# All projection weights of the last mixer as one sequence of tiles prepared two ahead, in four pairs of buffers

## The chip, the cores and the metric

The kernel runs on one core of a Trainium2 chip. The metric is the device time of one execution in microseconds (us); several runs give a median. Besides the times there is one profiled execution of the kernel before, with the start, the length and the releaser of the instructions of every engine: TensorE (PE in the profile; its weight loads are PEld), VectorE (DVE), ScalarE (ACT), GpSimd (POOL) and SyncE (SP), whose queue issues the DMAs.

## The reference, cut to what matters

The program computes two blocks on one sequence of 256 positions of width 1024, in fp32. The first block is a mixer and an MLP; the second has two layers, each a mixer and an MLP. The change touches the mixer of the very last layer, an RWKV-7 mixer:

```python
def _rwkv7_mixer(h, mu, w_rkv, w0, w_la, w_lb, a0, a_la, a_lb, g_la, g_lb,
                 k_k, k_a, r_k, ln_g, ln_b, w_o, v_first, v_mix):
    ...
    xx = jnp.pad(h, ((0, 0), (1, 0), (0, 0)))[:, :-1] - h
    xs = h[None] + xx[None] * mu[:, None, None, :]
    rkv = jnp.einsum('pbtd,pde->pbte', xs[:3], w_rkv)
    r, k, v = rkv[0], rkv[1], rkv[2]
    ...
    decay = jnp.exp(-jnp.exp(log_w.astype(f32)))
    ...
    a = jax.nn.sigmoid(a0 + (xa @ a_la) @ a_lb)
    g = jax.nn.sigmoid(xg @ g_la) @ g_lb
    kk = heads(k * k_k).astype(f32)
    kk = kk / jnp.maximum(jnp.sqrt(jnp.sum(kk * kk, axis=-1, keepdims=True)), 1e-12)
    k = k * (1.0 + (a - 1.0) * k_a)
    ...
    y = _wkv7_scan(r_h, heads(decay), k_h, v_h, kk, kk * heads(a).astype(f32))
    ...  # normalised per head, bonus added, times g
    return y.astype(h.dtype) @ w_o, v_first
```

The weights `w_rkv` are three 1024 x 1024 matrices, for r, k and v. The recurrence is computed in four windows of 64 positions, in two halves d = 0 and 1; inside a window a triangular system is solved by an elimination.

## The kernel before, in words

**Split arithmetic.** Every fp32 product is made of three matmuls on halves: a high half, which is the value rounded to the type fp32r, and a low half, which is the rest. `mm3` issues high x high, high x low and low x high (L227 to L229). A weight tile of 128 x 1024 goes through `split`: ACT writes the high half with a cast (L222), then DVE or POOL writes the low half with a subtraction (L223). In the names of the profile wk is the raw tile of a k weight, wkh and wkl its halves, and wr, wrh, wrl and wv, wvh, wvl the same for r and v; m1u, m2u and m3u are weights of the three MLPs. The pair of halves lies in one of two buffers of the pool `wp`; the raw 1 MB tile, which holds two split tiles, in one of two buffers of `wr`. A split can start when its raw tile has landed and the pair that it takes is no longer read by TensorE; a load can start when the raw buffer that it takes is no longer read by a split. Outside this mixer, `more_weights` lends two further pools, and then splits and loads alternate between the pools (the list `extra`).

**The last mixer** is the function `rwkv`. In its order of code: the input is normalised to hT by TensorE and ACT (rn, L1231 and L1235); xx is the difference to the position before (L1325); mixes of hT and xx are the inputs of the projections; `k_proj(0)` to `k_proj(3)` each load 256 columns of the k weights in one DMA, split them in two tiles and make two 128-column products, whose squares sq and their sums kk give the norms nk. `lora_b` loads the small matrix lwab into a raw buffer between `k_proj(0)` and `k_proj(1)`. After `k_proj(3)` an inverse square root over 128 x 32 values (`rsqrt`, L275 to L284, tiles nr and nt) gives the factors that ACT widens to ly (L1390) and TensorE turns into tile nk of PSUM (L1394); with them DVE and POOL make tA, tB and tK (tAR and tBK hold them). `r_proj(0)` and `r_proj(1)` stand between these steps; each `r_proj` ends in lx<-r and tAR<-r on DVE (L1414, L1415), the first two also in operations on tK.

**The elimination and its fill.** `blocks` makes the small blocks (AB), DVE solves them in 16 steps per half: in a step for half 0 DVE does the work, for half 1 POOL makes the product elp (`elp` = "dp", L921) and DVE adds it to hT (L924). Then come the pieces Pc, Zc, Rc and Uc on TensorE. While DVE eliminates, TensorE has its fill: the generator `dense` gives `r_proj(2)`, `r_proj(3)`, the bonus sums (bon, from pr, which is lx), and the eight tiles' v matmuls of the first half, `v_proj(0)`, with A (gram, L1469) between; `late` gives `v_proj(1)` and the gate (G). `v_out` writes V (L1529). At the end `fin` normalises the output per head (gv, gr, gt, tBK, L1699 to L1710), adds the bonus and multiplies by the gate; yt is its transpose for the product with `w_o`, yh and yl the halves of that, ra and res the residual sum, and then the last MLP starts with its weights m3u.

**Which engine splits.** The table `KP` names the engine of each low half: k "dd,dd,dd,dd" (all DVE), r "dp,pd,dd,pd" (POOL has r1, r2 and r6, counted from 0) and v "d,d,d,p,d,d,p,p" (POOL has v3, v6 and v7). The change leaves it as it is.

**What sets the order.** Each engine runs its instructions in the order that a scheduler has laid down when the program is built. It orders by priority and by when operands and buffers come free, so the place of a split in an engine's queue follows from the number of buffers too, and it is not the order of the code. An instruction that waits holds up all behind it on its engine.

## Time and profile before

| what | us |
|---|---|
| median of three runs | 1083.26 (1081.01, 1083.26, 1083.73) |
| the profiled execution | 1082.76 |
| its span in the trace | 1081.0 |
| PE busy in the span | 1044.6 (97%) |
| DVE busy | 734.9 (68%) |
| ACT busy | 553.0 (51%) |
| POOL busy | 71.2 (7%) |

The profiled execution took 1.8 us more than the span of its trace. The stage of the last mixer lies from about 620 to 880 us of the span. [...] A wait is put down to the releaser that came last; what that releaser was itself held up by has to be read from its engine.

### The profile page before, as it was taken

The numbers are of one execution on the slowest core, as the hardware profiler recorded it, in microseconds if no ns is written. First come the engines' busy times: TensorE is split into PE (matmuls) and PEld (weight loads), VectorE is DVE, ScalarE is ACT, GpSimd is POOL, SyncE is SP. The second block draws the span as 40 slices with busy tenths as digits, with TensorE's granted clock in tenths as the row PEclk, the third lists the DMA queues.
The fourth block names the chain that finished last, engine by engine and source line by source line (L and its number), as shares of the span: only waits on it lengthen the run. The fifth ranks groups of instructions, "written<-read, shape, count | busy, mean of one in ns | idle before, by whom it ended". The sixth has DMA issues, their size and how long they took to land.

```text
span 1081.0 us, 19651 instructions
## 1 busy us (share of the span) xinstructions
PE 1044.6 (97%) x8138; PEld 936.9 (87%) x8138; DVE 734.9 (68%) x1269; ACT 553.0 (51%) x826; POOL 71.2 (7%) x100
## 2 busy tenths in 40 slices
...
GB/s 245 122 157 118 45 343 196 195 162 189 160 211 139 215 157 194 160 172 185 156 273 194 179 154 47 98 105 92 60 99 112 86 156 158 193 195 187 187 133 40
DMA packets 113910, 169.44 MB, mean 157 GB/s; under 512 B 6446, under 2 KB 92443, under 8 KB 113564
## 3 DMA queue, kind: packets, MB, share of 16 engines
...
q8 instruction: 64, 1.05, 0.4%
...
q10 hardware_dynamic: 146, 0.07, 0.0%
HBM read 167.12 MB, written 1.05 MB: 156 GB/s over the span
## 4 chain that ended last, share of the span: by engine, by line
PE 82%; DVE 12%; ACT 3%; issue 2%; DMA 1%; POOL 1%; ACTq 0%; POOLq 0%; DVEq 0%
PE m1a L227 3%; PE m3h L228 3%; PE m3h L229 3%; PE m1a L229 3%; PE m1a L228 3%; PE m3h L227 3%; PE m1h L228 3%; PE m2h L228 3%; PE m2h L229 3%; PE m1h L229 3%; PE m1h L227 3%; PE m2h L227 3%; PE m2a L227 3%; PE m2a L228 3%; PE m2a L229 3%; PE m3a L227 3%
## 5 line engine op out<-in xcount | busy, mean ns | idle before, releaser
L227 PE MATMUL m1h<-m1xh,m1uh 128*128 128x256 f32 x256 | 73.4, 287 | 0.0
L229 PE MATMUL m3h<-m3xh,m3ul 128*128 128x256 f32 x256 | 72.3, 283 | 0.5 <-DVE m3ul L223 0.5
L228 PE MATMUL m3h<-m3xl,m3uh 128*128 128x256 f32 x256 | 72.2, 282 | 0.3 <-DVE m3xl L387 0.3
L227 PE MATMUL m3h<-m3xh,m3uh 128*128 128x256 f32 x256 | 72.1, 282 | 0.0
L228 PE MATMUL m1h<-m1xl,m1uh 128*128 128x256 f32 x256 | 71.9, 281 | 0.2 <-DVE m1xl L387 0.2
L229 PE MATMUL m2h<-m2xh,m2ul 128*128 128x256 f32 x256 | 71.7, 280 | 0.0
L229 PE MATMUL m1h<-m1xh,m1ul 128*128 128x256 f32 x256 | 71.7, 280 | 0.0
L228 PE MATMUL m2h<-m2xl,m2uh 128*128 128x256 f32 x256 | 71.7, 280 | 0.0
L223 DVE TENSOR_TENSOR m3ul<-m3u,m3uh 128x1024 fp32r<-128x1024 f32 x32 | 39.2, 1226 | 47.6 <-ACT m3uh L222 47.6
L227 PE MATMUL m2h<-m2xh,m2uh 128*128 128x256 f32 x256 | 71.6, 280 | 0.0
L223 DVE TENSOR_TENSOR m1ul<-m1u,m1uh 128x1024 fp32r<-128x1024 f32 x32 | 39.2, 1225 | 44.8 <-ACT m1uh L222 44.8
L223 DVE TENSOR_TENSOR m2ul<-m2u,m2uh 128x1024 fp32r<-128x1024 f32 x32 | 39.1, 1225 | 35.9 <-ACT m2uh L222 35.9
L222 ACT CAST m3uh<-m3u 128x1024 fp32r<-128x1024 f32 x32 | 33.5, 1047 | 53.9 <-PE m3h L228 50.0
L222 ACT CAST m1uh<-m1u 128x1024 fp32r<-128x1024 f32 x32 | 33.7, 1053 | 52.1 <-PE m1h L228 50.4
L222 ACT CAST m2uh<-m2u 128x1024 fp32r<-128x1024 f32 x32 | 33.5, 1050 | 47.9 <-PE m2h L228 45.4
L223 DVE TENSOR_TENSOR m2dl<-m2d,m2dh 128x1024 fp32r<-128x1024 f32 x32 | 39.2, 1224 | 26.1 <-ACT m2dh L222 26.1
L223 DVE TENSOR_TENSOR m3dl<-m3d,m3dh 128x1024 fp32r<-128x1024 f32 x31 | 38.0, 1225 | 24.9 <-ACT m3dh L222 24.9
L223 DVE TENSOR_TENSOR m1dl<-m1d,m1dh 128x1024 fp32r<-128x1024 f32 x31 | 37.9, 1224 | 22.0 <-ACT m1dh L222 22.0
L222 ACT CAST m2dh<-m2d 128x1024 fp32r<-128x1024 f32 x32 | 33.6, 1050 | 33.4 <-PE m2a L229 29.9
L222 ACT CAST m1dh<-m1d 128x1024 fp32r<-128x1024 f32 x31 | 32.5, 1047 | 35.3 <-PE m1a L229 24.4
L227 PE MATMUL m2a<-m2dh,m2fh 128*128 128x512 f32 x128 | 50.1, 391 | 0.0
L228 PE MATMUL m2a<-m2dl,m2fh 128*128 128x512 f32 x128 | 49.9, 390 | 0.0
...
## 6 DMA issues: line engine op xcount, KB each, us to landing
m1u<-in_w_up_dram SPq DMA_DIRECT2D x16, 1024.0 KB
m1d<-in_w_down_dram SPq DMA_DIRECT2D x16, 1024.0 KB, 4.9
m2u<-in_ffn_w_dram SPq DMA_DIRECT2D x16, 1024.0 KB, 6.6
m2d<-in_ffn_w_dram SPq DMA_DIRECT2D x16, 1024.0 KB, 5.6
m3u<-in_ffn_w_dram SPq DMA_DIRECT2D x16, 1024.0 KB, 5.6
m3d<-in_ffn_w_dram SPq DMA_DIRECT2D x16, 1024.0 KB, 4.8
win<-in_w_in_dram SPq DMA_DIRECT2D x10, 1024.0 KB
sv<-in_sgu_w_in_dram SPq DMA_DIRECT2D x8, 1024.0 KB, 6.9
```

Source lines behind the costliest of these rows:

```text
L222: act.copy(hv, src)
L223: lo.tensor_tensor(out=lv, in0=src, in1=hv.bitcast(F32), op=ALU.subtract)
L227: pe.matmul(out, lhsT=lh, rhs=rh, start=first, stop=False)
L228: pe.matmul(out, lhsT=lh, rhs=rl, start=False, stop=False)
L229: pe.matmul(out, lhsT=ll, rhs=rh, start=False, stop=last)
```

## The change

In `rwkv` a pool `wz` of two further pairs is opened and put on `extra` (with no raw pool beside it), so splits alternate between `wp` and `wz`, four pairs in all, until the end of `rwkv`, where it is popped. The SBUF for it is what `dynamic_dma_scratch_size=1024` gives up. The weights of k, r and v become one sequence of 24 tiles, k0 to k7, r0 to r7, v0 to v7. `prep(i)` loads and splits tile i (a raw tile for every second one); `tile_of(m, u, ahead)` prepares all tiles up to two beyond the one that is asked for (`k_proj(0)` asks with ahead=1) and returns it. Two further differences lie in the loads. A raw tile of k or r weights comes as two DMAs of 128 columns each in place of one of 256 columns; v weights come as four DMAs of 1 MB in place of eight of 512 KB. The branch for `lo == "x"` and the engine "x" are not reached, since `KP` names no "x".

```diff
--- before.py
+++ after.py
@@ -136,7 +136,7 @@
     act, dve, pool, pe, sync = nc.scalar, nc.vector, nc.gpsimd, nc.tensor, nc.sync
 
     cp = ctx.enter_context(tc.tile_pool(name="const", bufs=1))
-    EN = {"d": dve, "p": pool, "a": act}
+    EN = {"d": dve, "p": pool, "a": act, "x": "x"}
 
     def scale_by(e, out, in_, cols):
         if e is act:
@@ -178,7 +178,7 @@
 
     def raw(name):
         wpick[1] += 1
-        w_ = extra[-1][1] if extra and wpick[1] % 2 and not wpick[2] else wr
+        w_ = extra[-1][1] if extra and extra[-1][1] and wpick[1] % 2 and not wpick[2] else wr
         return w_.tile([P, 2048], F32, tag="raw", name=name)
 
     def load_ws(w, c0, name, n=256):
@@ -220,7 +220,11 @@
             hv = hv.rearrange("p (a b) -> p a b", a=shape[1])
             lv = lv.rearrange("p (a b) -> p a b", a=shape[1])
         act.copy(hv, src)
-        lo.tensor_tensor(out=lv, in0=src, in1=hv.bitcast(F32), op=ALU.subtract)
+        if lo == "x":
+            act.activation(out=lv, in_=hv.bitcast(F32), func=AF.Copy, scale=-1.0)
+            pool.dma_start(out=lv.bitcast(F32), in_=src, accum_op=ALU.add)
+        else:
+            lo.tensor_tensor(out=lv, in0=src, in1=hv.bitcast(F32), op=ALU.subtract)
         return hv, lv
 
     def mm3(out, lh, ll, rh, rl, first, last):
@@ -1143,7 +1147,38 @@
     def rwkv(fed, early, cols, mu, hcol, hka, laf):
         NP, CH = 8, 64
         half = 0.5 * DECAY
-        with tc.tile_pool(name="rw", bufs=1) as bp:
+        with tc.tile_pool(name="wz", bufs=2) as wz, tc.tile_pool(name="rw", bufs=1) as bp:
+            extra.append((wz, None))
+            w3 = a["rwkv_w_rkv_2"][0]
+            made, src = {}, {}
+            how = [KP[x].replace(",", "") for x in ("rk", "rr", "rv")]
+
+            def prep(i):
+                if i > 23 or i in made:
+                    return
+                m, u = divmod(i, 8)
+                if u % 2 == 0:
+                    t = raw(f"w{'krv'[m]}{u}")
+                    if m < 2:
+                        v = t.rearrange("p (j k c) -> p j k c", j=2, k=NK)
+                        for j in range(2):
+                            sync.dma_start(out=v[:, j], in_=w3[1 - m][:, (u + j) * P:(u + j + 1) * P]
+                                           .rearrange("(k p) c -> p k c", p=P))
+                        src[i], src[i + 1] = v[:, 0], v[:, 1]
+                    else:
+                        v = t.rearrange("p (j k c) -> p j k c", j=2, k=2)
+                        n, c = divmod(u, 4)
+                        sync.dma_start(out=t.rearrange("p (k c) -> p k c", k=4),
+                                       in_=w3[2][c * 256:c * 256 + 512, n * 512:n * 512 + 512]
+                                       .rearrange("(k p) c -> p k c", p=P))
+                        src[i], src[i + 1] = v[:, 0], v[:, 1]
+                made[i] = split(src.pop(i), "w" + "krv"[m], EN[how[m][u]])
+
+            def tile_of(m, u, ahead=2):
+                for i in range(8 * m + u + ahead + 1):
+                    prep(i)
+                return made[8 * m + u]
+
             nkeep = _O2["reset2"][0]
             cc = bp.tile([P, nkeep], F32, tag="cc2", name="cc2")
             sync.dma_start(out=cc, in_=a["c2"][:, :nkeep])
@@ -1201,7 +1236,6 @@
                 xx = xxf.rearrange("p (k t) -> p k t", k=NK)
                 mixf = m2.tile([P, 2, 1024], F32, tag="mix", name="mix", bufs=1)
                 sqf = m2.tile([P, 2, 512], F32, tag="sq", name="sq", bufs=1)
-                w3 = a["rwkv_w_rkv_2"][0]
 
                 xh, xl, _, part = fed
                 pool.memset(hT[:, :, 0:1], 0.0)
@@ -1286,8 +1320,7 @@
                 nk = mp.tile([P, 2, 2 * NP], F32, tag="nk", name="nk")
 
                 def k_proj(c, kh, kl):
-                    w = load_ws(w3[1], c * 256, f"wk{c}")
-                    hl = [split(w[:, :, j * P:(j + 1) * P], "wk", EN[KP["rk"].split(",")[c][j]]) for j in range(2)]
+                    hl = [tile_of(0, 2 * c + j, 2 if c else 1) for j in range(2)]
                     q = lin("k")
                     qv = q.rearrange("p (j t) -> p j t", j=2)
                     if c == 0:
@@ -1401,11 +1434,10 @@
                     EN[KP["tk"][1]].tensor_tensor(out=tK[:, s], in0=tK[:, s], in1=as4(tt[:, s]), op=ALU.mult)
 
                 def r_proj(c):
-                    w = load_ws(w3[0], c * 256, f"wr{c}")
                     q = lin("r")
                     qv = q.rearrange("p (j t) -> p j t", j=2)
                     for j in range(2):
-                        wh, wl = split(w[:, :, j * P:(j + 1) * P], "wr", EN[KP["rr"].split(",")[c][j]])
+                        wh, wl = tile_of(1, 2 * c + j)
                         for k in range(NK):
                             mm3(qv[:, j], wh[:, k], wl[:, k], rh[:, k], rl[:, k], k == 0, k == NK - 1)
                             if k % 2:
@@ -1510,9 +1542,7 @@
                     ac = gv[2]
                     m = slice(n * 512, n * 512 + 512)
                     for c in range(4):
-                        w = raw(f"wv{n}{c}")[:, :1024].rearrange("p (k c) -> p k c", k=2)
-                        sync.dma_start(out=w, in_=w3[2][c * 256:c * 256 + 256, m].rearrange("(k p) c -> p k c", p=P))
-                        wh, wl = split(w, "wv", EN[KP["rv"].split(",")[4 * n + c]])
+                        wh, wl = tile_of(2, 4 * n + c)
                         for j in range(2):
                             k = 2 * c + j
                             for t in range(2):
@@ -1798,6 +1828,7 @@
                     add_res(ac[1], 1, n, None)
                 for n in range(2):
                     fed[2](1, n)
+            extra.pop()
             return fed
 
     with more_weights(1, 1):
@@ -1876,7 +1907,7 @@
     import concourse.bacc as bacc
     from concourse.bass_utils import run_bass_kernel_spmd
 
-    nc = bacc.Bacc("TRN2", target_bir_lowering=False, num_devices=1)
+    nc = bacc.Bacc("TRN2", target_bir_lowering=False, num_devices=1, dynamic_dma_scratch_size=1024)
     arrays = {n: np.ascontiguousarray(inputs[n]) for n in _INS}
     arrays["c1"], arrays["c2"] = _C1, _C2
     arrays = {f"in_{n}_dram": v for n, v in arrays.items()}
```

What the diff alone does not show is how the queues stand afterwards. The lines of the kernel after are by 4 higher up to the head of `rwkv` and by 30 to 34 further down.

The first place is DVE's queue at the inverse square root nr, behind the last k projection. Before, from the first operation of the chain on:

```order
L284 TENSOR_SCALAR nr_7429<-nk_6995 128x32
L275 TENSOR_TENSOR nt_7430<-nr_7429 128x32
L276 TENSOR_TENSOR nt_7430<-nt_7430,nk_6995 128x32
L282 SCALAR_TENSOR_TENSOR nt_7430<-nt_7430 128x32
L282 SCALAR_TENSOR_TENSOR nr_7429<-nt_7430,nr_7429 128x32
L275 TENSOR_TENSOR nt_7430<-nr_7429 128x32
L1270 TENSOR_TENSOR mvl_7605<-mix_6824,mvh_7604 128x4x256
L276 TENSOR_TENSOR nt_7430<-nt_7430,nk_6995 128x32
L1414 TENSOR_TENSOR lx_6997<-r_7452,tBK_6809 128x512
L282 SCALAR_TENSOR_TENSOR nr_7429<-nt_7430,nr_7429 128x32
L1415 TENSOR_TENSOR tAR_6808<-r_7452,EL_6820 128x4x2x64
L223 TENSOR_TENSOR wrl_7554<-wr1_7522,wrh_7553 128x1024
```

After, at the same place; here the chain begins in the sixth row, and the splits are r3, r4 and r5 (the row tAR<-k and the mvl rows stood ahead of the rows shown before):

```order
L227 TENSOR_TENSOR wrl_7501<-wr2_7469,wrh_7500 128x1024
L1340 TENSOR_TENSOR tAR_6811<-k_7382,rwcols_5575 128x4x128
L1304 TENSOR_TENSOR mvl_7625<-mix_6827,mvh_7624 128x4x256 x2
L1349 TENSOR_SCALAR nk_6998<-kk_7434 128x2x4
L227 TENSOR_TENSOR wrl_7546<-wr4_7542,wrh_7545 128x1024
L288 TENSOR_SCALAR nr_7447<-nk_6998 128x32
L1446 TENSOR_TENSOR lx_7000<-r_7468,tBK_6812 128x512
L279 TENSOR_TENSOR nt_7448<-nr_7447 128x32
L1447 TENSOR_TENSOR tAR_6811<-r_7468,EL_6823 128x4x2x64
L280 TENSOR_TENSOR nt_7448<-nt_7448,nk_6998 128x32
L227 TENSOR_TENSOR wrl_7574<-wr4_7542,wrh_7573 128x1024
L286 SCALAR_TENSOR_TENSOR nt_7448<-nt_7448 128x32
```

Before, r3's split is the last row, behind the two operations that end r(0), and the chain has no split in it. Now r3, r4 and r5 stand in front of the chain and within it. TensorE's queue moves with it: ahead of its first nk it had, between the sums kk, 25 and 23 and 16 matmuls of r, and has now 33 and 15 and 41; the 48 matmuls of r(3) (24 a tile) now all stand before bon. Further up on DVE, k1's split, the product sel and k3's split stand ahead of xx, where k1 and sel stood, and k2 takes the place of k1; on ACT the casts of k1 and k3 stand before the first hT.

The second place is POOL's queue in the elimination; wvl are the splits of v tiles, elp the products of the steps 10 to 15 of half 1. Before:

```order
L921 TENSOR_TENSOR elp_8092<-elb_8073,hT_6822 128x16x10
L921 TENSOR_TENSOR elp_8131<-elb_8127,hT_6822 128x16x11
L223 TENSOR_TENSOR wvl_8227<-wv03_8224,wvh_8226 128x1024
L921 TENSOR_TENSOR elp_8176<-elb_8157,hT_6822 128x16x12
L921 TENSOR_TENSOR elp_8235<-elb_8211,hT_6822 128x16x13
L921 TENSOR_TENSOR elp_8260<-elb_8256,hT_6822 128x16x14
L921 TENSOR_TENSOR elp_8294<-elb_8284,hT_6822 128x16x15
L223 TENSOR_TENSOR wvl_8474<-wv12_8471,wvh_8473 128x1024
```

After:

```order
L925 TENSOR_TENSOR elp_8150<-elb_8146,hT_6825 128x16x11
L925 TENSOR_TENSOR elp_8195<-elb_8176,hT_6825 128x16x12
L227 TENSOR_TENSOR wvl_8321<-wv6_8318,wvh_8320 128x1024
L925 TENSOR_TENSOR elp_8252<-elb_8230,hT_6825 128x16x13
L925 TENSOR_TENSOR elp_8277<-elb_8273,hT_6825 128x16x14
L925 TENSOR_TENSOR elp_8311<-elb_8301,hT_6825 128x16x15
L227 TENSOR_TENSOR wvl_8405<-wv6_8318,wvh_8404 128x1024
```

Before, v3's split stands between the products 11 and 12, and v6's behind the last; now v3 stands behind the product 2 (further up than the rows shown), v6 between 12 and 13 and v7 behind the last. Also on POOL, r1 and r2 are now neighbours, and r6 stands ahead of the operations on tBK and xx that precede the elimination. On DVE the splits among the steps of the elimination were r7, v0, v1, v2 and v4 and are v0, v1, v2, v4 and v5, and the operations lx and tAR that end r(3) stand behind step 2, where they stood behind step 5. On TensorE 22 matmuls of v stand before the first piece of Pc, where 13 stood.

The third place is the end of `fin` on DVE, from the last product with V of one half to the last yl. Before:

```order
L1710 TENSOR_TENSOR tBK_6809<-tBK_6809,V1_7975 128x512
L275 TENSOR_TENSOR gt_9279<-gr_9278 128x8
L345 TENSOR_TENSOR res_79<-ra0_9266,res_79 128x512
L276 TENSOR_TENSOR gt_9279<-gt_9279,gv_9277 128x8
L345 TENSOR_TENSOR res_79<-ra0_9266,res_79 128x512
L282 SCALAR_TENSOR_TENSOR gr_9278<-gt_9279,gr_9278 128x8
L252 TENSOR_TENSOR yl_8842<-yt_9340,yh_8841 128x4x128
L1708 TENSOR_TENSOR tBK_6809<-tBK_6809,gr_9278 128x512
L1709 TENSOR_TENSOR tBK_6809<-tBK_6809,G1_7974 128x512
L1710 TENSOR_TENSOR tBK_6809<-tBK_6809,V1_7975 128x512
L223 TENSOR_TENSOR m3ul_9497<-m3u0_9494,m3uh_9496 128x1024
L252 TENSOR_TENSOR yl_8842<-yt_9359,yh_8841 128x4x128
```

After:

```order
L1739 TENSOR_TENSOR tBK_6812<-tBK_6812,G1_7995 128x512
L286 SCALAR_TENSOR_TENSOR gr_9281<-gt_9282,gr_9281 128x8
L349 TENSOR_TENSOR res_79<-ra0_9269,res_79 128x512
L1740 TENSOR_TENSOR tBK_6812<-tBK_6812,V1_7996 128x512
L1738 TENSOR_TENSOR tBK_6812<-tBK_6812,gr_9281 128x512
L349 TENSOR_TENSOR res_79<-ra0_9269,res_79 128x512
L1739 TENSOR_TENSOR tBK_6812<-tBK_6812,G1_7995 128x512
L256 TENSOR_TENSOR yl_8845<-yt_9343,yh_8844 128x4x128
L1740 TENSOR_TENSOR tBK_6812<-tBK_6812,V1_7996 128x512
L256 TENSOR_TENSOR yl_8845<-yt_9362,yh_8844 128x4x128
L227 TENSOR_TENSOR m3ul_9505<-m3u0_9498,m3uh_9504 128x1024
```

The split of m3u0's first tile, which stood between the two yl, is no longer in the rows: it stands further up, between gv and gr of the last normalisation. The row below the second yl is the split of m3u0's second tile. A res row now stands before V.

## Rows read from the trace of the kernel before

**Rows 1.** The chain that ended last, share of the span by engine.

```profile
PE 82%; DVE 12%; ACT 3%; issue 2%; DMA 1%; POOL 1%; ACTq 0%; POOLq 0%; DVEq 0%
```

**Rows 2.** TensorE's waits, 620 to 900: engine, line, releaser: us, times, longest.

```profile
PE A L1469 <- DVE lx L1473: 2.4, 1, 2.4
PE nk L1394 <- ACT ly L1390: 1.6, 1, 1.6
...
PE v L227 <- DVE V L1529: 1.3, 2, 0.7
PE kk L1314 <- ACT sq L1310: 1.1, 1, 1.1
PE r L229 <- POOL wrl L223: 0.9, 1, 0.9
PE k L229 <- DVE wkl L223: 0.8, 1, 0.8
...
PE yt L248 <- DVE gt L275: 0.4, 1, 0.4
```

**Rows 3.** Windows: length; busy PE, PEld, DVE, ACT, POOL; clock, DMA, GB/s.

```profile
720.00:740.00 20.00, 17.36 (x366) 16.15 (x367) 19.73 (x32) 7.66 (x12) 5.14 (x5) 1.00 0.31 98
728.00:732.00 4.00, 4.00 (x36) 4.00 (x36) 3.97 (x7) 1.88 (x4) 0.00 (x0) 1.00 0.76 251
752.00:756.00 4.00, 4.00 (x22) 3.94 (x21) 1.89 (x15) 0.00 (x0) 0.86 (x3) 0.57 0.70 228
760.00:780.00 20.00, 17.65 (x132) 14.01 (x131) 19.41 (x59) 10.69 (x27) 5.83 (x8) 0.99 0.25 80
```

**Rows 4.** Tile wk: its splits, shortest/mean/longest in ns, from and to.

```profile
L222 ACT CAST wkh<-wk x8: 1039/1052/1056, 651.8 to 707.2; 128x1024 fp32r<-128x1024 f32 x8
L223 DVE TENSOR_TENSOR wkl<-wk,wkh x8: 1202/1220/1254, 652.9 to 709.9; 128x1024 fp32r<-128x1024 f32 x8
```

**Rows 5.** Timeline of DVE: start, length, line, operation, idle time before.

```profile
720.08 2.31 DVE L275 TENSOR_TENSOR nt<-nr 128x32 f32<-128x32 f32 x1
722.42 0.19 DVE L276 TENSOR_TENSOR nt<-nt,nk 128x32 f32<-128x32 f32 x1
...
739.81 2.85 DVE L1574 TENSOR_TENSOR hT<-xx,cc 128x512 f32<-128x512 f32 x1
...
756.50 0.69 DVE L1414 TENSOR_TENSOR lx<-r,tBK 128x512 f32<-128x512 f32 x1 [2.57 <-PE r L229]
...
772.21 3.05 DVE L924 TENSOR_TENSOR hT<-hT,elp 128x176 f32<-128x176 f32 x2
```

**Rows 6.** Timeline of POOL: two weight splits.

```profile
719.97 2.38 POOL L223 TENSOR_TENSOR wrl<-wr,wrh 128x1024 fp32r<-128x1024 f32 x1
...
794.77 2.37 POOL L223 TENSOR_TENSOR wvl<-wv,wvh 128x1024 fp32r<-128x1024 f32 x1 [7.79 <-ACT wvh L222]
```

**Rows 7.** Timeline of TensorE: first and last of 20 matmuls of k.

```profile
704.43 0.28 PE L227 MATMUL k<-mkh,wkh 128*128 128x256 f32 x1
...
706.66 0.28 PE L228 MATMUL k<-mkl,wkh 128*128 128x256 f32 x1
```

**Rows 8.** Timeline of TensorE: first and last of 15 matmuls of 512 columns.

```profile
639.80 0.39 PE L227 MATMUL m2a<-m2dh,m2fh 128*128 128x512 f32 x1
...
642.97 0.39 PE L229 MATMUL m2a<-m2dh,m2fl 128*128 128x512 f32 x1
```

**Rows 9.** Timeline of DVE at xx, ahead of the k projections.

```profile
669.87 1.23 DVE L1325 TENSOR_TENSOR xx<-hT 128x1024 f32<-128x1024 f32 x1 [2.40 <-ACT hT L1235]
```

**Rows 10.** Timeline of ACT at its first hT.

```profile
666.00 2.17 ACT L1235 ACTIVATE hT<-rn,gcols 128x128 f32<-128x128 f32 x8 [2.80 <-PE rn L1231]
```

**Rows 11.** Timeline of DVE in fin.

```profile
869.81 0.17 DVE L284 TENSOR_SCALAR gr<-gv 128x8 int32<-128x8 int32 x1
...
873.37 0.69 DVE L1710 TENSOR_TENSOR tBK<-tBK,V 128x512 f32<-128x512 f32 x1
```

**Rows 12.** DMA from 518 to 523.6, and issues from 620 to 830: KB, us.

```profile
DMA packets 3120, 1.05 MB, mean 187 GB/s; under 512 B 2096, under 2 KB 3120, under 8 KB 3120
...
wk<-in_rwkv_w_rkv_dram SPq DMA_DIRECT2D x4, 1024.0 KB, 5.1
```

## Prediction

> **What bounds the kernel now.** The chain of work that ended last comes first: TensorE holds 82% of it, DVE 12% [rows 1], so only time in which TensorE stands still, or runs slower, can be won. All edits lie in the last mixer, so I read TensorE's waits from 620 to 900 us [rows 2]. Two name a weight split: k<-DVE wkl (0.8 us) and r<-POOL wrl (0.9). Four more up to the end of v_out(0) name neighbours: nk<-ACT ly 1.6, kk<-ACT sq 1.1, A<-DVE lx 2.4, v<-DVE V 1.3. The stretches say why: DVE is busy 19.73 of 20 us from 720 to 740 and 19.41 from 760 to 780 [rows 3]; there TensorE waits for DVE's queue, whatever name the last releaser has. So the second question is what lengthens that queue. First, splits of 1.22 us [rows 4]. Second, instructions held up beside POOL: nt<-nr, a 128x32 operation, takes 2.31 us against 0.19 for its successor, hT<-xx 2.85 against 0.69 for an lx<-r of the same size, hT<-hT 3.05 for two [rows 5]; a POOL split of about 2.4 us runs beside the first, and its like beside the others [rows 6]. Third, a stop of 2.57 us before lx<-r [rows 5], where DVE's head waits for the r projection.
>
> A matmul of a k or r projection starts every 0.117 us (20 of them, 704.43 to 706.66) [rows 7], one of 512 columns every 0.226 (15, 639.80 to 642.97) [rows 8].
>
> **The change, part by part.** I write k0 to v7 for the 24 split tiles. Engines, sizes and numbers of splits and matmuls stay the same; no engine is spared work, it only moves.
>
> *Splits ahead of the stage.* k1 and k3 now stand on DVE around sel, before xx. DVE was idle for 2.40 us there [rows 9], and two splits are 2 x 1.22 = 2.44; ACT, which casts them before its first hT, was idle 2.80 us [rows 10]. So k3 costs nothing, nor does k1, which stood a little earlier, and k2 takes k1's old place. If that cover is short, xx and all behind it are late by some tenths. From there each split position of the k projections holds the tile two further on, so DVE's packed part begins with two splits fewer: -2.4 us. k6's split is done long before its matmuls, so the 0.8 of [rows 2] goes: -0.8. The load of lwab, in k1's raw buffer, now waits for k1's split, and its cast stands behind the hT and mix casts on ACT: 0.
>
> *The nr chain* (first order fence). r3, r4 and r5 stand in or before it, where r3 followed it. Ahead of the first nk TensorE now has 33+15+41 = 89 matmuls of r instead of 25+23+16 = 64: 25 x 0.117 = 2.9 us of work in place of the waits of 0.9 and 1.6. That counts only if the nr chain comes no later. For it: r2's POOL split, beside which nt<-nr lost 2.31 - 0.19 = 2.1 [rows 5], is ready earlier. Against it: r1 and r2 then run beside the two lv instructions and r3. I take half, -1.0; bounds 0 and -2.1. ACT's casts of r4 to r6 stand before the ly copies and wait for buffers: r6's for r2's, free after 24 of the 41 matmuls, so it ends before ly is due.
>
> *The elimination.* From the first AB evacuation to the last transposes DVE does v0, v1, v2, v4, v5 where it did r7, v0, v1, v2, v4; against the two splits taken off at the start, the packed part holds one more at its end (v5): +1.2. POOL's r6 now runs before the AB evacuation, so the 2.85 - 0.69 = 2.2 that hT<-xx lost [rows 5] goes, unless r6 hits the tA and tB work instead; half, -1.1 (0 to -2.2). The 2.57 stop goes if r(3) is done when lx comes: TensorE has the 0.8 + 0.9 + 1.6 = 3.3 us from above in hand and does all of r(3) before bon, but lx also stands three steps earlier; -2.0 (0 to -2.6). POOL's v6, which ran at 794.77 with DVE out of its way [rows 6], now stands between elp 12 and elp 13 (second fence). Its nearest row is v3, in the same kind of place: hT<-hT took 3.05 for two [rows 5]. So at most it costs the length of a POOL split, 2.4 [rows 6], in which POOL's next elp waits too; at least 0.3, a little overlap. I take 2.3, nearest to v3. v3 itself moves from step 11 to step 2, at its old price.
>
> Sum on DVE at the end of the elimination: -2.4 - 0.8 + 1.2 - 1.0 - 1.1 - 2.0 + 2.3 = -3.8. The best bounds give -8.6, but TensorE can't win more than its waits there, 0.8 + 0.9 + 1.6 + 2.4 + 1.3 = 7.0; the worst give +0.4.
>
> *Before Pc.* Nine v matmuls that stood between the Pc and Zc pieces come ahead of the first Pc, so TensorE fills with them what it would wait for X: 9 x 0.226 = 2.0, -2.0. It is 0 if the pieces behind then lack cover; eight or more v matmuls still stand before Zc, so I take -2.0. Together -5.8 of the 7.0.
>
> *fin and m3u0.* w_out's splits 2 and 3 now take one pair from either pool, so m3u0's first split finds a buffer early, and DVE's queue gets it, 1.22 as in [rows 4], between gv and gr of the last normalisation. DVE has no gap there from gr at 869.81 to V at 873.37 [rows 11], and TensorE already waits 0.4 for yt [rows 2]: yt comes 1.2 later, later again by the res operation that now stands before V (0.69, as V's last [rows 11]) (third fence), and yl behind further operations. Against that, m3ul is there later on. I take +1.8, bounds 0 and +2.4.
>
> *DMA.* k and r weights come as two loads of 128-column pieces, in rows of 512 bytes where one load had 1024. Landing took 5.1 us for 1 MB [rows 12]; at twice the packets the bound is 10.2. The nearest row is the load of la: 1.05 MB in 3120 packets, 2096 of them under 512 bytes, all between 518 and 523.6 us [rows 12]; so 5.1 to 6. The tightest is r6: its load can start once r3 is split, 1.05 + 1.22 = 2.3 us [rows 4] after the last k matmul; its cast is due 72 r matmuls after that, 72 x 0.117 = 8.4; 6.1 us of room, so nothing waits. The scratch given up holds nothing of this kernel, which starts no DMA on POOL's queue: 0.
>
> [...]
>
> **Sum.** 1082.76 (the profiled execution; the median is 0.5 above it) - 3.8 - 2.0 + 1.8 = 1078.8.
>
> **Rivals.**
> *Given back on DVE:* the waits named by weights go, but the packed queue, with v6 inside and r1, r2 beside lv, ends where it ended, and the waits come back as A<-DVE and Pc<-DVE: 0 - 2.0 + 1.8: 1082.6. For it: no DVE work is saved, 19.73 of 20 [rows 3]. Against: two splits and the 2.57 stop do leave it.
> *No weight is late:* TensorE's two weight waits are 1.7 us in all [rows 2]; if only they go and fin costs 1.8, 1082.9. I count it with the last.
> *Late landing, slower:* if 1 MB in 512-byte rows takes over 6.1 us, r6's cast heads ACT's queue ahead of ly, and nk waits. At 10.2 it is 4.1 late, about 7 with r4's load on the same queue still running when r6's starts; that is some 4 beyond TensorE's extra 2.9 of work. DVE's -3.8 turns to about +2.9; then -2.0 + 1.8; and the clock, at 0.57, mostly its lower level, from 752 to 756, lets through 22 matmuls where 728 to 732 has 36 [rows 3], (36 - 22) x 0.117 = 1.6 more after such a stop: 1087. Against it stands the load of la.
> *More:* if that stretch at 0.57 goes as well, all 7.0 are won and fin is free: -7.0 - 1.6: 1074.2.
>
> **How the numbers follow.** Forecast 0.60 (1075.5 to 1081.5), given back and no weight late 0.24, slower 0.09, more 0.07. A measurement of this kernel tells about 0.3% from no change, 3.25 us: faster ends at 1080.0, slower begins at 1086.5. Some four fifths of the forecast lie below 1080.0: 0.49 + 0.07 = 0.56 faster; 0.09 slower; 0.35 within. The range leaves out the slower rival and most of the last one: 1074.8 to 1084.4.
>
> **What would show it.** Right: no wait on wkl or wrl; first nk with no wait; DVE's last transposes of the elimination 3 to 5 us earlier; a POOL wvl between two elp with DVE held up beside it; yt<-DVE at 1.5 to 2 us near the end. Wrong: casts waiting for a DMA, an nr chain as late as before, lx<-r still stopping DVE, or Pc waiting over 3 us for DVE.

## The result, and the profile after

The changed kernel is slower. Its median is 1093.24 us (four runs, 1091.22 to 1094.80) against 1082.76 for the kernel before (1081.01 to 1083.73); the ratio is 1.0095, with a 95% interval of 1.0079 to 1.0112. The forecast was 1078.8, with a range of 1074.8 to 1084.4 and a chance of 0.09 for slower; the median lies 8.8 us above that range. The profiled execution of the changed kernel took 1091.22 us (span 1089.4), that of before 1082.76 (span 1081.0). Four single runs of the experiments below were disturbed and took 2584 to 3851 us (one each of before, e7, e9 and e15); they stand in no ratio, and in a median they count for less than 0.1 us.

The medians differ by 10.5 us, the two profiled executions by 8.5. Nothing happens outside the last mixer. I cut both traces at the same instructions of TensorE: the last m2a, the first AB (the elimination begins), the first Pc, the last Zc, the first Rc, the first yt of `fin` and the first m3h of the MLP. Between the cuts, in us:

| part | before | after | difference |
|---|---|---|---|
| last m2a to first AB (projections, nr chain) | 73.83 | 77.10 | +3.27 |
| first AB to first Pc (elimination) | 57.42 | 56.20 | -1.22 |
| first Pc to last Zc | 17.73 | 19.14 | +1.41 |
| last Zc to first Rc | 8.50 | 8.37 | -0.13 |
| first Rc to first yt | 42.14 | 43.57 | +1.43 |
| first yt to first m3h (`fin`) | 30.74 | 34.81 | +4.07 |
| sum | 230.36 | 239.19 | +8.83 |

The parts do not hold the same work. Of the 192 matmuls of r, 101 stand ahead of the first AB before and 117 after, and of the 96 of v, 58 and 67 stand ahead of the first Pc. At 0.117 us for one of r and 0.226 for one of v [rows 7, 8], 1.9 us of work moved from the second part to the first, and 2.0 from the third to the second. For the same work, then, the differences of the first three parts are about +1.4, -1.4 and +3.4. And one execution is a coarse measure: e1_fin, e3_v7_dve and e4_v_between_pc (below) have the changed kernel's order on every engine up to the first AB, and their first parts took 75.7, 75.5 and 78.1.

TensorE's waits of the changed kernel from 620 to 910, releaser, us, times and longest, answer to [rows 2]:

```profile
PE kk L1347 <- ACT sq L1343: 3.6, 2, 2.4
PE Pc L1621 <- issue: 2.5, 1, 2.5
PE Pc L1621 <- DVE xx L1614: 2.2, 1, 2.2
PE yt L252 <- DVE tBK L1740: 1.9, 1, 1.9
PE v L231 <- DVE V L1559: 1.8, 1, 1.8
...
PE A L1501 <- DVE lx L1505: 0.2, 1, 0.2
```

What the change was made for did happen. The waits on wkl (0.8) and wrl (0.9) and nk<-ACT ly (1.6) are gone, and A<-DVE lx fell from 2.4 to 0.2: 5.5 us of waiting won. But kk<-ACT sq grew from 1.1 to 3.6, v<-DVE V from 1.3 to 1.8, yt's from 0.4 to 1.9, and two stops before and in Pc are new, 2.2 and 2.5: 9.2 lost.

In the part from the first Rc to the first yt, which grew by 1.4, a stop before Uc without a releaser lasted 1.4 in place of 0.7, and Uc waited 0.6 for sq.

The second loss is not in a list of waits. These are stretches of the changed kernel (length; busy PE, PEld, DVE, ACT, POOL; granted clock of TensorE as a share of full speed, DMA share, GB/s), to be read beside [rows 3]:

```profile
716.00:720.00 4.00, 1.55 (x14) 1.35 (x13) 4.00 (x10) 1.67 (x3) 0.40 (x1) 1.00 0.30 73
720.00:724.00 4.00, 4.00 (x20) 4.00 (x20) 2.30 (x4) 0.33 (x1) 0.00 (x0) 0.50 0.88 238
724.00:728.00 4.00, 4.00 (x25) 4.00 (x24) 3.61 (x8) 1.05 (x1) 1.27 (x1) 0.64 0.00 2
796.00:800.00 4.00, 2.33 (x41) 1.55 (x41) 0.20 (x1) 0.00 (x0) 0.00 (x0) 0.50 0.01 4
880.00:884.00 4.00, 3.20 (x10) 2.10 (x11) 2.98 (x5) 0.59 (x1) 0.00 (x0) 0.56 0.00 0
884.00:888.00 4.00, 4.00 (x14) 3.29 (x13) 1.92 (x2) 1.53 (x2) 0.00 (x0) 0.59 0.37 90
```

From 716 to 720 TensorE works 1.55 of 4 us, and in the 8 us behind that the granted clock is 0.50 and 0.64: it is never idle there, but 20 and 25 matmuls pass where the kernel before passes 36 at 1.00 [rows 3]. The same follows the stop in Pc and the one before yt. Summed as (1 - clock) x 4 us over the stretches of 4 us from 660 to 904, before lacks 12.0 us of full clock and after 20.5. I take that as an upper bound on what the clock cost, since it counts waits within such stretches as well. Weighted with the time that TensorE was busy it is 11.1 and 18.4, 7.3 more; but that too may be more than it cost: in `fin` below, 3.4 us of lacking clock cost about 2.2. So waits and clock make up the 8.8 together: all idle time of TensorE between the cuts, named here or not, grew from 15.6 to 20.2 us, 4.6, and its matmuls were busy for 219.0 us in place of 214.8, 4.2 more for the same work.

### The profile page after: what moved, and what is told of

Same layout as the page of the kernel before. It is cut to its first block, busy times and chain, and to the rows that moved or that the text cites. A ratio compares the mean times of both kernels' runs of the same rounds, so it can differ in the third digit from the quotient of the medians.

```text
span 1089.4 us, 19653 instructions
## 1 busy us (share of the span) xinstructions
PE 1049.8 (96%) x8138; PEld 940.9 (86%) x8138; DVE 736.5 (68%) x1269; ACT 552.7 (51%) x826; POOL 72.2 (7%) x100
## 4 chain that ended last, share of the span: by engine, by line
PE 82%; DVE 11%; ACT 2%; issue 2%; DMA 1%; POOL 1%; SPq 0%; ACTq 0%; POOLq 0%; DVEq 0%
PE m1a L231 3%; PE m3h L232 3%; PE m3h L233 3%; PE m1a L233 3%; PE m1a L232 3%; PE m3h L231 3%; PE m1h L232 3%; PE m2h L232 3%; PE m2h L233 3%; PE m1h L233 3%; PE m2h L231 3%; PE m1h L231 3%; PE m2a L231 3%; PE m2a L232 3%; PE m2a L233 3%; PE m3a L231 3%
## 5 line engine op out<-in xcount | busy, mean ns | idle before, releaser
L232 PE MATMUL m3h<-m3xl,m3uh 128*128 128x256 f32 x256 | 72.1, 282 | 0.3 <-DVE m3xl L391 0.3
L231 PE MATMUL m3h<-m3xh,m3uh 128*128 128x256 f32 x256 | 72.1, 282 | 0.0
L222 ACT CAST m3uh<-m3u 128x1024 fp32r<-128x1024 f32 x32 | 33.6, 1049 | 51.7 <-PE m3h L232 51.7
L222 ACT CAST m2dh<-m2d 128x1024 fp32r<-128x1024 f32 x32 | 33.6, 1050 | 33.4 <-PE m2a L233 28.1
```

What stands on the lines that cost most here:

```text
L222: act.copy(hv, src)
L231: pe.matmul(out, lhsT=lh, rhs=rh, start=first, stop=False)
L232: pe.matmul(out, lhsT=lh, rhs=rl, start=False, stop=False)
```

## The experiments

From this trace I named four causes: **POOL's hold-up** (r1 and r2 run back to back beside small DVE operations, so kk is late and the clock falls), **v7** (POOL's last v split beside the last elimination step), **Pc in one run** (the nine v matmuls moved ahead leave 186 Pc matmuls without anything between) and **fin** (m3u0's split ahead of gr). The rival was that the sequence or the four pairs of buffers cost by themselves. A ratio compares the runs of a kernel with those of the kernel before that were taken beside them; it is not the quotient of two medians. The intervals of e1 to e4 overlap that of the changed kernel, so none of these four shows its part by its time alone; the table at the end has the stage lengths of each.

### fin

e1_fin gives the two added buffers back just before `w_out`:

```diff
                 for n in range(2):
                     fed[2](1, n)
-            extra.pop()
             return fed
...
+                extra.pop()
                 wo_raw = []
                 f00, f01 = fin(0, 0), fin(0, 1)
```

> The changed kernel, but the extra pool of pairs is taken off the list just ahead of the loads of w_out, so fin and the first tile of m3u0 stand on DVE as in the kernel before; all else is the changed kernel. In the changed kernel the stretch from the first yt (864.43) to the first m3h (899.24) lasts 34.8 us; in the kernel before 860.06 to 890.80, 30.7 us. Theory 1 (m3u0's split between gv and gr delays yt by over a microsecond, TensorE stops 1.9 + 0.7 us, its clock falls, and the products after it run at half speed): the stretch goes back to about 30.7, the wait yt<-DVE to about 0.4, and the time falls by 4 us, to about 1089. Rival (the stretch is long because what comes before it arrives later and thinner, whatever the place of the split): the stretch stays above 33.5 and the time within 1 us of the changed kernel.

Measured: 1089.68, 1.0066 (1.0044 to 1.0088). The part `fin` returns from 34.81 to 30.75 (30.74 before). DVE in the changed kernel, at the place of [rows 11] (start, length, line, operation, idle time before):

```profile
873.99 0.16 DVE L1735 TENSOR_SCALAR gv<-gv 128x8 f32<-128x8 f32 x1
874.07 1.22 DVE L227 TENSOR_TENSOR m3ul<-m3u,m3uh 128x1024 fp32r<-128x1024 f32 x1
875.20 0.16 DVE L288 TENSOR_SCALAR gr<-gv 128x8 int32<-128x8 int32 x1
```

TensorE at yt, the changed kernel first:

```profile
880.12 0.79 PE L252 MATMUL yt<-ident,tBK 128*128 128x128 f32 x4 [1.90 <-DVE tBK L1740]
881.59 0.80 PE L231 MATMUL ra<-rwoh,yh 128*128 128x512 f32 x1 [0.68 <-ACT yh L255]
882.19 0.63 PE L232 MATMUL ra<-rwol,yh 128*128 128x512 f32 x1
882.61 0.63 PE L233 MATMUL ra<-rwoh,yl 128*128 128x512 f32 x1
```

and e1_fin:

```profile
879.97 0.63 PE L252 MATMUL yt<-ident,tBK 128*128 128x128 f32 x4 [0.32 <-DVE gt L279]
```

The split stands where the order said, and TensorE waits 1.5 us longer for yt than before. Then 512-column matmuls start 0.43 apart instead of 0.226 [rows 8]; from 880 to 888 the clock is 0.56 and 0.59, in e1_fin 1.00. Where the same split stands in the same place and yt waits as long, but the clock stays at 1.00 (e3_v7_dve, e13_r1r2_cut and e14_r3r4r5_cut, below), the part is 32.5 to 32.6: 1.8 over before. So 1.8 is the wait and what follows from it, and some 2.2 more is half clock. The time agrees: 3.6 us less than the changed kernel, where 4 were expected.

### POOL's hold-up

e2_r1r2_dve puts r1 and r2 on DVE; nothing else changes:

```diff
-'rr': 'dp,pd,dd,pd'
+'rr': 'dd,dd,dd,pd'
```

> The changed kernel with r1 and r2 split on DVE and not on POOL. In the changed kernel POOL's two neighbouring splits run from 708.4 to 715.1, and DVE's lv, lam and hT<-cc operations beside them take 5.4 us longer than in the kernel before; kk waits 2.4 us for sq, and TensorE's clock is 0.50 to 0.64 from 720 to 728. Theory 1 (DVE held up beside POOL is what makes nr late): DVE has two splits more, 2 x 1.22 = 2.4, but the 5.4 go, so nr starts about 3 us earlier than 722.1, the kk wait shrinks below 1 us, the half-speed stretch goes, the first AB comes 2 to 3 us earlier than 737.2, and the time falls by 2 to 4 us. Rival (what counts is the work that stands in DVE's queue ahead of tAR<-k and nr, splits that were moved there): two more splits make nr 2.4 us later, kk waits longer, and the time rises by 2 us or more.

Measured: 1091.24, 1.0082 (1.0063 to 1.0101); the first part took 75.72, which lies within the 75.5 to 78.1 of the four executions that leave that part as it is, so nothing is shown to be won. The kk wait of 2.4 is gone, but with two more splits in DVE's queue nk<-ACT ly waits 2.1. The hold-up itself is plain in the changed kernel; DVE, to be read beside [rows 5]:

```profile
707.84 5.04 DVE L1413 SCALAR_TENSOR_TENSOR lv<-lv 128x1024 f32<-128x1024 f32 x2
...
712.87 2.32 DVE L1414 COPY lam<-EL 128x32 f32<-128x32 f32 x1
715.12 1.64 DVE L1606 COPY hT<-cc 128x256 f32<-128x256 f32 x2
...
716.90 1.23 DVE L227 TENSOR_TENSOR wrl<-wr,wrh 128x1024 fp32r<-128x1024 f32 x1
718.04 0.68 DVE L1340 TENSOR_TENSOR tAR<-k,rwcols 128x512 f32<-128x512 f32 x1
...
722.12 0.17 DVE L288 TENSOR_SCALAR nr<-nk 128x32 int32<-128x32 int32 x1
724.32 0.69 DVE L1446 TENSOR_TENSOR lx<-r,tBK 128x512 f32<-128x512 f32 x1 [2.03 <-PE r L233]
```

POOL beside it, which answers to [rows 6]:

```profile
708.43 6.72 POOL L227 TENSOR_TENSOR wrl<-wr,wrh 128x1024 fp32r<-128x1024 f32 x2
715.11 1.29 POOL L1434 TENSOR_TENSOR tBK<-tBK,lx 128x512 f32<-128x512 f32 x1
```

DVE in the kernel before, the same operations with no POOL split beside them:

```profile
708.22 1.71 DVE L1380 SCALAR_TENSOR_TENSOR lv<-lv 128x1024 f32<-128x1024 f32 x1
...
711.19 1.23 DVE L1380 SCALAR_TENSOR_TENSOR lv<-lv 128x1024 f32<-128x1024 f32 x1
712.33 0.18 DVE L1381 COPY lam<-EL 128x32 f32<-128x32 f32 x1
...
713.67 0.49 DVE L1576 COPY hT<-cc 128x256 f32<-128x256 f32 x2
```

TensorE:

```profile
719.45 1.36 PE L1347 MATMUL kk<-cc,sq 128*128 128x2 f32 x8 [2.45 <-ACT sq L1343]
```

POOL needs 6.72 us for the two splits instead of 2 x 2.38 [rows 6], and lam, a copy of 128x32 that takes 0.18 in the trace before, takes 2.32 and ends at 715.19, when POOL's second split ends (708.43 + 6.72 = 715.15). Taken singly, the two engines take turns: the first split ends at 711.79, the second lv at 712.88, the second split at 715.14 and lam at 715.20. The same five operations (two lv, lam, two hT) took 1.71 + 1.23 + 0.18 + 0.49 = 3.61 us before and take 9.0 now (of the 5.4 more, 1.2 fall on hT beside POOL's tBK). Then r3's split stands ahead of tAR, from which ACT makes sq; kk starts at 719.45 instead of 717.32, and nr at 722.12 instead of 718.97. What makes either engine wait for the other is not shown.

e13_r1r2_cut keeps the changed kernel's order on every engine and shortens the two POOL splits to 16 of 128 columns; e14_r3r4r5_cut does the same with DVE's r3, r4 and r5, and there the order behind nr changes somewhat. What is left out: the low halves of these tiles; the high half stands in for them in the matmuls, so all matmuls remain.

```diff
-            lo.tensor_tensor(out=lv, in0=src, in1=hv.bitcast(F32), op=ALU.subtract)
-        return hv, lv
+            c = slice(0, 16) if cut else slice(None)
+            lo.tensor_tensor(out=lv[..., c], in0=src[..., c], in1=hv.bitcast(F32)[..., c], op=ALU.subtract)
+        return (hv, hv) if cut else (hv, lv)
...
-                made[i] = split(src.pop(i), "w" + "krv"[m], EN[how[m][u]])
+                made[i] = split(src.pop(i), "w" + "krv"[m], EN[how[m][u]], cut=i in (9, 10))
```

For e14_r3r4r5_cut the list is (11, 12, 13).

> The changed kernel in which POOL's splits of r1 and r2 cover 16 columns of 128 only, and TensorE takes the high halves of these two tiles in place of the low ones (so the two low halves are left out of the product). Every engine's order is that of the changed kernel. Theory 1 (operations of DVE are held up while a POOL split runs): lv, lam and hT<-cc on DVE take 1.2, 0.2 and 0.4 us each in place of 5.04 for two, 2.32 and 1.64, nr starts 3 to 4 us earlier, kk waits less than 0.5 us, the stretch at half speed at 720 goes, and the first AB comes about 73 us after the last m2a in place of 77.1 (75.6 at least in the others of this order). Rival (r3's and r4's splits ahead of nr are the cause): 75 us or more, kk still waiting over 1.5 us.

> The changed kernel in which the splits of r3, r4 and r5 on DVE cover 16 columns of 128 only, and TensorE takes their high halves in place of the low ones (three low halves are left out of the product). The scheduler then sets a somewhat different order behind nr. POOL's r1 and r2 are whole. DVE has about 3 us less to do ahead of the first nk. Theory 1 (hold-up beside POOL, then TensorE's stop and its clock): kk still waits 1 us or more, and the first AB comes 74.5 us or more after the last m2a. Rival (the three splits ahead of nr are the cause): kk waits less than 0.5 us and the first AB comes at 73.5 us or less.

Measured: 1091.72, 1.0093 (1.0066 to 1.0120), and 1092.13, 1.0081 (1.0061 to 1.0101). Neither is shown to win anything. In e13_r1r2_cut the hold-up is gone, but DVE then stands before r3's split for ACT's cast, and a later POOL split (r6) catches the nr chain. Its DVE:

```profile
710.35 3.22 DVE L1414 SCALAR_TENSOR_TENSOR lv<-lv 128x1024 f32<-128x1024 f32 x2
...
713.58 0.37 DVE L1415 COPY lam<-EL 128x32 f32<-128x32 f32 x1
...
716.87 1.23 DVE L228 TENSOR_TENSOR wrl<-wr,wrh 128x1024 fp32r<-128x1024 f32 x1 [2.24 <-ACT wrh L222]
...
726.87 2.30 DVE L287 SCALAR_TENSOR_TENSOR nr<-nt,nr 128x32 f32<-128x32 f32 x1
```

and its POOL:

```profile
726.76 2.36 POOL L228 TENSOR_TENSOR wrl<-wr,wrh 128x1024 fp32r<-128x1024 f32 x1 [1.89 <-ACT wrh L222]
```

nr<-nt,nr is 128x32, 0.19 elsewhere, and ends with POOL's split: the same hold-up as nt<-nr's 2.31 before [rows 5], moved. The kk wait falls from 3.6 to 1.1 and the clock stays 1.00 from 708 to 728, yet nk now waits 2.3, the clock is 0.82 and 0.75 from 728 to 736, and the first part is 77.33. In e14_r3r4r5_cut kk still waits 3.5 and the clock is 0.57 from 720 to 724; nr comes at 719.86, but the first part, 75.89, holds 100 matmuls of r and not 117; behind it TensorE stops 3.1 us before an r matmul, again without a releaser. POOL's r6 meets tBK:

```profile
730.63 2.86 DVE L1432 SCALAR_TENSOR_TENSOR tBK<-lv,tAR 128x512 f32<-128x512 f32 x1
```

So my theory that one hold-up explains the first part fell. The waits suggest at least two limits in a row, POOL's hold-up and the splits and casts that stand ahead of nr, where freeing one hands the end to the next. No run shows that by its time: e4_v_between_pc, whose first part is the changed kernel's, had both waits in one execution, kk 2.5 and nk 2.2.

### v7

e3_v7_dve moves v7's split from POOL to DVE:

```diff
-'rv': 'd,d,d,p,d,d,p,p'
+'rv': 'd,d,d,p,d,d,p,d'
```

> The changed kernel with v7 split on DVE, where it stands behind the last transposes of the elimination, and not on POOL, where it ran beside the last step: hT<-hT took 2.92 us there for two, and TensorE's first piece of Pc waited 2.2 us for DVE's xx. Theory 1 (that POOL split is what ends the elimination late): hT<-hT falls to about 0.8, the wait Pc<-DVE to about 0.2, the first Pc comes 2 us earlier than 793.35, and the time falls by about 2 us. Rival (the 2 us come back further on, as v7's halves come later or as TensorE meets the next wait at its instruction stop in Pc): the first Pc comes earlier, but the last Zc and the time move by less than 0.7 us.

Measured: 1090.40, 1.0073 (1.0056 to 1.0090). The wait of Pc for xx (2.2) is gone, and the elimination takes 55.12 instead of 56.20. In the changed kernel, DVE at v3 and at the last step:

```profile
752.98 3.43 DVE L928 TENSOR_TENSOR hT<-hT,elp 128x32 f32<-128x32 f32 x2
...
789.08 2.92 DVE L928 TENSOR_TENSOR hT<-hT,elp 128x240 f32<-128x240 f32 x2
```

POOL there:

```profile
788.85 2.57 POOL L227 TENSOR_TENSOR wvl<-wv,wvh 128x1024 fp32r<-128x1024 f32 x1
```

The split of v7 sits beside the two hT of the last step, on the path over xx to Pc. All v splits on DVE (e10_v_all_dve, below) bring the part to 53.20.

### Pc in one run

e4_v_between_pc gives back v matmuls between the Pc pieces:

```diff
-'fl': [4, 4, 4, 2, 4, 2, 16, 8]
+'fl': [2, 4, 4, 2, 4, 2, 16, 8]
```

> The changed kernel with the first value of the table fl at 2 and not 4, so that three matmuls of v each come between the pieces of Pc's second half already (before the first Pc stand the same 19 v matmuls). In the changed kernel TensorE ran 186 little matmuls of Pc without a break and then stood still for 2.5 us with no releaser but issue. Theory 1 (a long run of little matmuls uses up the instructions that TensorE has at hand, and the next portion of 16 KB on the instruction queue is late): the run is about half as long, the stop falls below 0.5 us, and the last Zc comes about 2 us earlier than 812.49, if the v matmuls that are missing further on are not missed; time about 2 us less. Rival (the stop belongs to this place of the program, whatever stands between): the stop stays at 2 to 2.5 us, the time within 1 us.

Measured: 1091.81, 1.0079 (1.0063 to 1.0095). The stop in Pc is gone, but the one before Uc grew from 1.4 to 2.6: part of it moved. From the first Pc to the first yt, which hold the same matmuls in both, e4 takes 68.5 us and the changed kernel 71.1 (e1, e2 and e3, with that order, 70.8 to 72.1), so some 2.6 were won there; what stands ahead of the first Pc is unchanged and took 2.7 longer in this one execution. First the changed kernel's Pc:

```profile
793.35 1.79 PE L1621 MATMUL Pc<-xx 32*32 32x32 f32 x186 [2.18 <-DVE xx L1614]
797.67 0.33 PE L1621 MATMUL Pc<-xx 32*32 32x32 f32 x6 [2.53 <-issue]
```

TensorE's longest wait of e4_v_between_pc from 785 to 840:

```profile
PE Uc L1654 <- issue: 2.6, 1, 2.6
```

### The sequence and the buffers apart

e5_sequence_two_pairs keeps the sequence without the added buffers:

```diff
-        with tc.tile_pool(name="wz", bufs=2) as wz, tc.tile_pool(name="rw", bufs=1) as bp:
-            extra.append((wz, None))
+        with tc.tile_pool(name="rw", bufs=1) as bp:
...
-            extra.pop()
             return fed
```

e6_four_pairs_no_sequence is the kernel before with the added buffers, given back before `w_out` as in e1_fin:

```diff
-        with tc.tile_pool(name="rw", bufs=1) as bp:
+        with tc.tile_pool(name="wz", bufs=2) as wz, tc.tile_pool(name="rw", bufs=1) as bp:
+            extra.append((wz, None))
...
```

e7_three_pairs is e1_fin with one added pair:

```diff
-        with tc.tile_pool(name="wz", bufs=2) as wz, tc.tile_pool(name="rw", bufs=1) as bp:
+        with tc.tile_pool(name="wz", bufs=1) as wz, tc.tile_pool(name="rw", bufs=1) as bp:
...
```

> The changed kernel without the pool wz: the sequence of 24 tiles prepared two ahead and its new loads, but only the two pairs of the kernel before. In DVE's queue no split of r then stands within the chain of nr, m3u0's first split stands where it stood before, and v7 stands on POOL behind the last step of the elimination. Theory 1 (the loss comes from the splits that the two added pairs let stand early): the time from the last m2a to the first AB is about 73.8 us as in the kernel before (75.6 to 78.1 in the changed kernel and in those of the first four runs that leave that part as it is), from the first yt to the first m3h 30.7 us, and the time lies within 2 us of the kernel before, 1082.7. Rival (the sequence itself costs, by its loads in rows of 512 bytes or by the order of the preparations): 1086 or more, with the casts of r waiting for a DMA.

> The kernel before with the two added pairs of the pool wz, taken off the list ahead of w_out as in the first run, and without the sequence: each projection loads and splits its own tiles as before. In DVE's queue r3 and r4 don't stand ahead of nr, r3 stands within its chain; POOL's r1 and r2 have an operation on tBK between them; v6 stands on POOL between steps 13 and 14, v7 behind the last; 12 matmuls of v stand ahead of the first Pc. Theory 1 (what stands ahead of nr decides the first part, a POOL split in the steps and TensorE's long run of Pc the second): the first AB comes 73.8 to 75 us after the last m2a, and the time is 1083 to 1087, between the kernel before and the first run (1089.7). Rival (four pairs cost whatever the order, as more splits run beside each other): the first AB comes as late as in the changed kernel, 75.6 or more, and the time is 1088 or more.

> The kernel of the first run (the changed kernel with fin as before) with one added pair in place of two. The splits of r3, r4 and r5 then stand behind the head of nr's chain on DVE, POOL has tBK between r1 and r2, and v6 runs on POOL two steps earlier, v7 behind the last step. Theory 1 (the splits ahead of nr and beside the last steps make the loss, not the sequence): the first AB comes 73.8 to 75 us after the last m2a, kk waits less than 1.5 us, and the time is 1083 to 1086. Rival (the later places bring other stops of the same size): 1088 or more.

> The kernel of the seventh run once more, for a profile that can be read. Its times there were 1089 to 1094, about those of the changed kernel, where 1083 to 1086 were expected. Theory 1 (three pairs bring the splits behind nr, but other waits of TensorE for splits): the first AB about 74 us after the last m2a, and the loss in the part from AB to Pc, 59 us or more (57.4 in the kernel before). Rival (the first part stays late as well): first AB after 75.6 us or more.

Measured: e5 1089.26, 1.0053 (1.0036 to 1.0069); e6 1097.81, 1.0139 (1.0123 to 1.0154); e7 1093.6, 1.0093 (1.0069 to 1.0117). The trace of the three pairs is that of e12_three_pairs_look, the kernel of e7 once more (1089.37). TensorE's waits of e5_sequence_two_pairs:

```profile
PE k L233 <- DVE wkl L227: 2.2, 2, 1.4
PE r L233 <- POOL wrl L227: 1.9, 1, 1.9
PE A L1500 <- DVE lx L1504: 1.7, 1, 1.7
```

and of e6_four_pairs_no_sequence:

```profile
PE v L227 <- DVE V L1530: 6.0, 1, 6.0
PE kk L1315 <- ACT sq L1311: 3.9, 2, 2.9
```

In all three the time came out as the rival said, though in e5 no cast waits for a DMA. Each half costs by itself, and not the same way. With two pairs the sequence makes the weight waits larger (0.8 and 0.9 before), at a clock as high as before (12.0 us lacking). Four pairs without the sequence are the slowest of all: V (6.0) and sq (3.9) come late; that what the splits displace is waited for is my reading, and I did not follow that order further. Three pairs are no better than four (k waits 1.2 and r 1.3 on their splits again). So the added pairs do take away the sequence's weight waits. That the rest of the loss is in the order that comes with both is argued, by the corrections below, and not shown by these runs.

### Corrections put together

All of these start from e1_fin. e15_all_r3_pool has

```diff
-'fl': [4, 4, 4, 2, 4, 2, 16, 8]
+'fl': [2, 8, 4, 2, 4, 2, 16, 8]
...
-'rr': 'dp,pd,dd,pd'
-'rv': 'd,d,d,p,d,d,p,p'
+'rr': 'dp,dp,dd,pd'
+'rv': 'd,d,d,d,d,d,d,d'
```

Of the others, e8_r2_v7_dve has r2 and v7 on DVE and r3 too (`'dp,dd,dd,pd'`, `'d,d,d,p,d,d,p,d'`) and the old `fl`; e9_r3_pool is e8 with r3 on POOL; e10_v_all_dve is e9 with all v on DVE; e11_v_between_pc_2 is e9 with the new `fl`; e16_all_r3_dve has `'dp,dd,dd,pd'`, `'d,d,d,d,d,d,p,d'` and the new `fl`.

> The kernel of the first run (1089.7) with r2 and v7 split on DVE and not on POOL; r1, r6, v3 and v6 stay on POOL. Theory 1 (each POOL split beside DVE's operations with two inputs from SBUF costs DVE about as much as it saves; v7's was 2.1 us on the end of the elimination, r1 and r2 together 5.4 us for two splits of 1.2): Pc<-DVE falls from 2.2 to about 0, kk from 2.4 to about 1.5, and the time is 2 to 4 us below the first run, about 1086.5. Rival (the stop of TensorE in Pc for its instructions and its half-speed stretch absorb it): 1089 to 1090.

> The kernel of the eighth run (1085.6; fin as before, r2 and v7 on DVE) with r3 split on POOL and not on DVE. DVE then has no split between the first operation of k7's norm, tAR<-k, and the work ahead of it (there r3's split took 2.23 us beside POOL), and the head of nr stands ahead of r4's split; 80 rows of Pc stand in one run and not 96. Theory 1 (a split in DVE's queue ahead of tAR<-k makes kk, and so TensorE and its clock, late): kk waits less than 0.5 us in place of 1.3, there is no half-speed stretch at 720 to 724, the first AB comes about 73.5 us after the last m2a (74.4 in the eighth run, 73.8 in the kernel before), the time falls by 1 to 2 us. Rival (r1 and r3 as neighbours on POOL hold DVE and tBK<-tBK,lx up instead): kk on time, but lx<-r or nr late, first AB at 75 us or more, the time the same or above 1085.6.

> The kernel of the ninth run with v3 and v6 on DVE too, so that no POOL split of v runs beside the elimination. In the eighth run POOL's v3 held hT<-hT of steps 1 and 2 up to 3.43 us for two and v6 the operations of step 12 by about 1 us; two splits on DVE cost 2.4. By TensorE's order 13 matmuls of v stand ahead of the first Pc and v matmuls come after 64 rows of Pc, not 96. Theory 1 (POOL splits beside the elimination cost DVE as much as they take off it): from the first AB to the first Pc 55.6 us or less as in the eighth run, the stop with no releaser but issue in Pc falls from 2.0 to below 0.7, and the time is 1 to 3 us below the ninth run. Rival (two more splits on the queue that ends the elimination): first AB to first Pc 56.5 us or more, and the time equal or above.

> The kernel of the ninth run with the first two values of the table fl at 2 and 8 in place of 4 and 4: v matmuls come after 40 rows of Pc already, and then between the pieces, with as many left for the pieces of Zc as can be had. Theory 1 (the stop in Pc comes from the length of the run of little matmuls; in the fourth run it went, but came back in Uc, where the matmuls that had been moved were missing): the stop in Pc goes (2.0 in the eighth run), a stop in Uc stays under 1 us, and the time is 1 to 2 us below the ninth run. Rival (it only moves): stops of 2 us or more in Zc or Uc, and the time within 1 us of the ninth run.

> The kernel of the eleventh run (1083.6) with v3 and v6 split on DVE as in the tenth. If the gains add up: first AB to first Pc 53.2 us as in the tenth run (54.2 in the eleventh), first Pc to last Zc 16.4 as in the eleventh, the rest as in the eleventh, and the time about 1 us below it, 1082 to 1083, about the kernel before. Rival (they don't add up, since the wait v<-DVE V or a stop in Uc grows): 1084 or more.

> The kernel of the eighth run (1085.6: fin as before, r2, r3 and v7 on DVE) with the values 2 and 8 at the head of the table fl as in the eleventh, and v3 on DVE too; v6 alone is left on POOL among the v tiles. If the gains add up: the first AB 74.4 us after the last m2a as in the eighth run (75.3 in the eleventh), first AB to first Pc 54 us, first Pc to last Zc about 17, and the time 1 to 3 us below the eleventh run, 1081 to 1082.5, a little under the kernel before (1082.8). Rival (the first part is spread by TensorE's clock more than by the place of r3): 1083.5 or more.

Measured, with the parts of the table above (us, from one profiled execution each) and the full clock lacking from 660 to 904:

| kernel | median | ratio (95%) | to AB | to Pc | to Zc | to Rc | to yt | fin | clock |
|---|---|---|---|---|---|---|---|---|---|
| before | 1082.76 | | 73.8 | 57.4 | 17.7 | 8.5 | 42.1 | 30.7 | 12.0 |
| after | 1093.24 | 1.0095 (1.0079-1.0112) | 77.1 | 56.2 | 19.1 | 8.4 | 43.6 | 34.8 | 20.5 |
| e1 | 1089.68 | 1.0066 (1.0044-1.0088) | 75.7 | 57.5 | 21.0 | 8.4 | 42.6 | 30.8 | 18.8 |
| e2 | 1091.24 | 1.0082 (1.0063-1.0101) | 75.7 | 57.6 | 18.9 | 8.4 | 43.6 | 33.6 | 20.5 |
| e3 | 1090.40 | 1.0073 (1.0056-1.0090) | 75.5 | 55.1 | 19.7 | 8.4 | 44.0 | 32.6 | 18.8 |
| e4 | 1091.81 | 1.0079 (1.0063-1.0095) | 78.1 | 57.9 | 20.4 | 2.4 | 45.7 | 34.8 | 18.7 |
| e5 | 1089.26 | 1.0053 (1.0036-1.0069) | 76.5 | 59.4 | 17.1 | 8.5 | 43.1 | 30.8 | 12.0 |
| e6 | 1097.81 | 1.0139 (1.0123-1.0154) | 79.9 | 62.3 | 17.6 | 8.4 | 44.0 | 30.7 | 18.8 |
| e12 | 1089.37 | one run | 78.7 | 58.1 | 16.7 | 9.3 | 42.1 | 30.8 | 12.0 |
| e13 | 1091.72 | 1.0093 (1.0066-1.0120) | 77.3 | 58.6 | 19.1 | 8.4 | 44.0 | 32.6 | 20.5 |
| e14 | 1092.13 | 1.0081 (1.0061-1.0101) | 75.9 | 60.1 | 19.8 | 8.4 | 44.1 | 32.5 | 20.5 |
| e8 | 1085.56 | 1.0024 (1.0008-1.0040) | 74.4 | 55.6 | 18.3 | 11.0 | 42.3 | 30.8 | 18.8 |
| e9 | 1087.56 | 1.0024 (1.0006-1.0042) | 75.4 | 56.6 | 19.5 | 11.0 | 42.7 | 30.8 | 20.5 |
| e10 | 1086.74 | 1.0028 (1.0016-1.0041) | 75.4 | 53.2 | 19.4 | 11.0 | 42.4 | 30.7 | 15.3 |
| e11 | 1083.64 | 1.0004 (0.9988-1.0020) | 75.3 | 54.2 | 16.4 | 8.8 | 42.8 | 30.8 | 10.3 |
| e15 | 1081.53 | 0.9982 (0.9969-0.9995) | 75.4 | 53.6 | 15.8 | 8.8 | 41.7 | 30.8 | 10.2 |
| e16 | 1081.85 | 0.9989 (0.9977-1.0001) | 74.4 | 55.6 | 18.5 | 8.8 | 41.7 | 30.7 | 15.4 |

The first part holds 101 matmuls of r before, 117 or 118 in after, e1 to e4, e8, e13 and e16, 114 in e9 to e11 and e15, and 115, 107, 119 and 100 in e5, e6, e12 and e14.

Against what was expected: e8 came out with its theory (2 to 4 us below e1), and so did e11, whose stop in Pc is 0.4. e9's first AB and time are its rival's, later than in e8 and no lower, but kk is not on time either: it waits 2.3. e10 brings the elimination to 53.2, but its stop in Pc is still 1.1, V is waited for by 3.9, and its time is e9's. e15 is a little better than expected, and e16 as expected in time but not in its parts.

Together the corrections take back all of the loss and a little more: e15_all_r3_pool is 0.18% faster than before, by an interval that ends just under 1. It keeps the sequence and the four pairs, and changes only which engine splits what, when the buffers go back, and the spread of v among Pc. So these three together are enough to make up the loss. Whether they undo it, or win what the kernel before would win by them too, is not shown: no run gives the kernel before the other engines or the new `fl`. From after over e1, e8 and e11 to e15 the ratio falls step by step; of the neighbours in this row only e1 and e8 have intervals that do not overlap, so the share of each correction is not shown. The profiled execution of e15 is its fastest run (1078.34), so its parts flatter it by some 3 us. Its first part is 1.6 over before, but it holds 13 more matmuls of r (114 in place of 101), 1.5 us, so for the same work it is where it was. e8 and e16, with 117, took 74.4 each, about 1.3 under before for the same work. So what the idea was for, earlier splits for k and r, paid at most that much. From AB to the last Zc e15 is 5.7 shorter, of which those 13 matmuls are 1.5; there A<-DVE lx no longer waits and v has no split on POOL, while V is waited for by 3.9 (1.3 before).

## Why the prediction was wrong, step by step

**Splits ahead of the stage (-2.4, -0.8).** The wait on wkl went, as told. The 2.4 did not arrive: DVE's packed part does begin with two splits fewer, but the five operations from lv to hT take 5.4 us more, and nr comes 3.2 late.

**The nr chain (-1.0, bounds 0 and -2.1).** This is the first step that failed: the term for r1 and r2 beside the lv instructions. I saw that r1 and r2 would run beside the lv instructions and netted that against nt<-nr's 2.1. The gain is there: nt<-nr takes 0.18 (2.31 in [rows 5]). The price was mis-sized: at most 2.1 by my bounds, and 5.4 as measured. Two POOL splits in a row hold DVE up until 715.2, the second lv by 2.2 and lam by 2.1. That price was in the rows: a whole POOL split of 2.4 for each 128x32 operation that meets one [rows 5, 6], two times. And I did not follow the chain to its next link: tAR feeds sq, sq feeds kk, and the next r matmuls stand behind kk on TensorE, so it waits 2.45 us. "25 x 0.117 = 2.9 us of work in place of the waits" came true for nk (no wait), and kk took the wait instead. Up to here -2.4, -0.8 and -1.0 were forecast; the first part of the trace is 1.4 longer for the same work.

**The elimination (-1.1, -2.0, +2.3, +1.2).** The two hT<-xx fell from 2.85 + 0.69 to 0.92 + 1.41, so by 1.2, and the 2.57 us stop before r(3)'s lx is gone: both as told. But a stop of 2.0 before r(0)'s lx, at 724.32, is new. v3 cost as much at step 2 as at step 11 (one hT of 2.20, where one took 2.51 before). v6 cost about 1, not 2.3. The miss is v7: I placed it "behind the last" product and gave it no price, but it holds up the last two hT, 2.92 where the two of the step before take 0.69; e3_v7_dve takes that wait of Pc away. The part is 1.2 shorter, with nine v matmuls (2.0 us) moved into it and sixteen of r (1.9) out of it.

**Before Pc (-2.0).** The second step that failed. I asked only whether the pieces behind would lack cover. Nineteen v matmuls run without a stop up to 791.17, yet the first Pc still waits 2.18 for xx, which the hT beside v7 make late. And it leaves Pc as one run of 186 matmuls at 1.79 us, and then TensorE stands for 2.53 us, for which the profile shows no releaser. Part Pc to Zc is 1.4 longer, with 2.0 us of work less: where 2.0 were to be won, nothing was, and 1.4 were lost. e11_v_between_pc_2, which spreads Pc further, has 0.4 of that stop and 16.4 us.

**fin (+1.8).** Place and mechanism right, the term mis-sized: 4.07. The wait and what follows from it are 1.8, as the runs at full clock show; the half clock behind it was not in the term.

**DMA (0).** Right. The loads wk and wr of the changed kernel (KB each, median us to landing):

```profile
wk<-in_rwkv_w_rkv_dram SPq DMA_DIRECT2D x8, 512.0 KB, 4.8
wr<-in_rwkv_w_rkv_dram SPq DMA_DIRECT2D x8, 512.0 KB, 4.1
```

Before, one load of 1 MB took 5.1 and 6.3. The last packets of a pair of 512 KB loads for r, which make one buffer, end 5.0 to 5.5 us after the issue of the first, and no cast waits for a DMA. So the slower rival came out by another mechanism than the one that I gave it. One term of it was right, the clock after a stop (1.6), and it belonged into the main sum: behind the waits that this change added, at 720, 796 and 880, the granted clock was 0.50 for 6.7 us and more.

**The sum.** The main sum had no term for the clock. By the trace it is about half of the loss: idle time grew by 4.6 us, and 4.2 are the same matmuls taking longer, while the clock lacks 7.3 to 8.5 us more. That is one execution, and the clock alone is no explanation: e5, with the clock of before, loses 6 by other waits, and e8, with nearly the lack of the changed kernel (18.8), loses 2.6. Not settled: how the first part divides between POOL's hold-up, the casts and the clock; and why e1_fin spreads over 7.8 us in six runs, where before spread over 3.9 in eleven runs beside it.
